# Sharing the last post norm between four engines, and loading x in smaller parts: one encoder layer on one core

## The chip, the cores and the metric

One core of one Trainium2 chip runs the kernel. The metric is the device time of one execution in microseconds (us), lower is better. TensorE is PE in the profile, VectorE is DVE, ScalarE is ACT, GpSimd is POOL, and SyncE, which only issues DMAs here, is SP. ACT issues some DMAs too.

## What is computed

```python
def layer_norm(x, g, b):               # over the last axis, float32, eps 1e-5
    mu, var = mean(x), mean((x - mu) ** 2)
    return (x - mu) * rsqrt(var + eps) * g + b

h = layer_norm(x, emb_ln_g, emb_ln_b)            # x: 256 tokens x 4096
p = h @ w_in                                     # 4096 x 13312
y_conv = c_b * centred_short_conv(c_c * c_h, conv_w) * silu(c_z)      # parts of p
y_attn = banded_window_attention(a_q, a_k, a_v, sink) * silu(a_z)     # parts of p
y = concat([y_conv, y_attn]) @ w_out             # 4096 x 4096
out = layer_norm(2 ** 0.25 * h + y, ln_g, ln_b)
```

## The kernel before

The 256 tokens are two tiles of 128, i = 0 and 1, with tokens on the partitions. The weights of both projections stream in as pieces of 1 MB; ACT rounds each to its high part (`split_hi`, L197), DVE subtracts to get the low part (`split_lo`, L201), and PE multiplies three times per piece (high by high, high by low, low by high).

**Prologue (L281 to L437).** x is loaded in parts of columns (`x_load`), and between the loads of the two tiles stand two pieces of w_in (`first`, `load(0)` and `load(1)`). DVE takes statistics per 512 columns (`stats`, L311), closes them (`stats_end`), normalises (`norm`, L319); PE turns the tiles (`transp`, L326, `transp2`, L344), ACT applies scale and shift (`turned1`, L332), and PE multiplies the turned x by the first two pieces in full float32 (`first_mm`, L361). All engines work through their instructions in the order in which the code issues them. On ACT the order is: the square root of tile 1, `split_hi(2)`, then `turned1(1, 0)`. On PE: the turns of tile 1 (L326, L344), then `first_mm(0, 1)`.

**The norm's small steps** are `small_chain` (L267 to L279): ACT takes a square root, DVE a reciprocal and one Newton step, and the last two instructions leave 1/sigma in `dst[.., 2]` and -mu/sigma in `dst[.., 3]`.

**The end (L978 to L992).** R (128 x 2 x 4096, in SBUF) holds alpha * h + y, and, for all chunks of columns that are done, already times ln_g (`end_out2`, L892). The last chunk has 256 columns; PE finishes it for tile 0 first, so that the norm of tile 0 runs while PE works on tile 1. For one tile: `finish_lhs` adds the residual, takes the statistics, calls `small_chain` and writes -mu/sigma, in a high and a low part and beside ones, to t5 (L900 to L905); `finish_tr` turns t5 on PE (L910) and copies it to lhs5 on ACT (L911); `finish_out` has, for each 512 columns, one matmul with 5 rows on PE that makes the shift -mu/sigma * ln_g + ln_b in PSUM (L918), and one instruction on DVE, R / sigma + shift (L919). Stores go out from L923 in pairs of 512 columns, the last two singly, from SP and ACT in turn.

`res_load` (L841 to L845) loads the rows that the residual of a chunk needs, for the last chunk into a tile z; it stands ahead of the load of the last piece of w_out.

Of the kernel before, what the change touches and what calls it, by code (L numbers as in the profile page):

```python
# [11 lines left out]
ALU = mybir.AluOpType  # L12
# [82 lines left out]
def encoder_kernel(ctx: ExitStack, tc: tile.TileContext, x, emb_g, emb_b, wi, ws, conv_w, sink, wo, ln_g, ln_b, out):  # L95
# [170 lines left out]

    def small_chain(dst, w):  # L267

        sd = small.tile([P, w], F32, name="sd", bufs=1)
        nc.scalar.activation(sd, dst[:, :, 1], AF.Sqrt, bias=eps_t)  # L270
        v = small.tile([P, w], F32, name="v", bufs=1)
        nc.vector.tensor_scalar(v, dst[:, :, 1], LN_EPS, -0.5, op0=ALU.add, op1=ALU.mult)
        y0 = small.tile([P, w], F32, name="y0", bufs=1)
        nc.vector.reciprocal(y0, sd)
        t = small.tile([P, w], F32, name="t", bufs=1)
        nc.vector.tensor_tensor(t, y0, y0, op=ALU.mult)
        nc.vector.tensor_tensor(t, t, v, op=ALU.mult)
        nc.vector.scalar_tensor_tensor(dst[:, :, 2], t, 1.5, y0, op0=ALU.add, op1=ALU.mult)
        nc.vector.scalar_tensor_tensor(dst[:, :, 3], dst[:, :, 0], -1.0, dst[:, :, 2], op0=ALU.mult, op1=ALU.mult)  # L279

    with tc.tile_pool(name="pro", bufs=1) as pro:  # L281
        warm = small.tile([P, 1], F32, name="sd", bufs=1)
        nc.scalar.activation(warm, eps_t, AF.Sqrt)
        xs = [pro.tile([P, D], F32, name=f"x{i}") for i in range(2)]
# [3 lines left out]

        def x_load(i):
            for c0, c1 in ((0, 1024), (1024, 2048), (2048, 3072), (3072, 3584), (3584, 4096)):  # L290
                nc.sync.dma_start(out=xs[i][:, c0:c1], in_=x[i * P:(i + 1) * P, c0:c1])

        first = [wpool.tile([P, PIECE], F32, name=f"first{j}", tag="whi") for j in range(2)]
# [13 lines left out]
        NQ = KT // 4  # L307
        st = [pro.tile([P, NQ, 6], F32, name=f"st{i}") for i in range(2)]

        def stats(i, c):  # L310
            nc.vector.bn_stats(st[i][:, c, :], xs[i][:, c * 512:(c + 1) * 512])  # L311

        def stats_end(i):
            nc.vector.bn_aggr(musd[:, i, 0:2], st[i])
            small_chain(musd[:, i:i + 1, :], 1)

# [40 lines left out]

        def first_mm(q, i):
            for k in range(PK):
# [8 lines left out]

        for c in range(NQ):
            stats(0, c)  # L370
# [13 lines left out]
        for c in range(NQ):  # L384
            stats(1, c)
        transp2(2, (0,))
        transp2(3, (0,))
        stats_end(1)
        split_hi(2)
# [409 lines left out]
    def open_p2():  # L799
        nonlocal p2, R, st2, ms2, rows, t5, lhs5  # L800
        ph.close()
        phs.close()
        p2 = ctx.enter_context(tc.tile_pool(name="p2", bufs=1))
        R = p2.tile([P, 2, D], F32, name="R")
        st2 = [p2.tile([P, ncs, 6], F32, name=f"s2{i}") for i in range(2)]
        ms2 = p2.tile([P, 2, 4], F32, name="ms2")
        rows = p2.tile([P, 3 * W], F32R, name="rows")
        t5 = p2.tile([P, 2, 72], F32, name="t5")
        nc.vector.memset(t5, 0.0)
        for b in (0, 32, 64):  # L810
# [19 lines left out]
    def res_load(n):  # L830
# [63 lines left out]
    def finish_lhs(n, i):  # L894
        r = end_out(n, i)
        nc.vector.bn_aggr(ms2[:, i, 0:2], st2[i])
        small_chain(ms2[:, i:i + 1, :], 1)
        ch = small.tile([P, 1], F32R, name="ch", bufs=1)
        c = ms2[:, i, 3:4]
        nc.vector.tensor_copy(ch, c)  # L900
        nc.vector.tensor_tensor(t5[:, i, 1:2], c, ch.bitcast(F32), op=ALU.subtract)
        for b in (0, 32, 64):
            if b:
                nc.vector.tensor_copy(t5[:, i, b + 1:b + 2], t5[:, i, 1:2])
            nc.vector.tensor_copy(t5[:, i, b:b + 3:2], ch.bitcast(F32).to_broadcast([P, 2]))  # L905
        end_out2(n, i, r)

    def finish_tr(i):
        tp = ps_att.tile([P, P], F32, name="att")
        nc.tensor.transpose(tp[0:72, :], t5[:, i, :], ident)  # L910
        nc.scalar.activation(lhs5[0:69, i, :], tp[0:69, :], AF.Copy)  # L911

    def finish_out(i, cs):
        for c in cs:
            sl = slice(c * 512, (c + 1) * 512)
            sh = (ps_att if c % 2 else ps_p).tile([P, 512], F32, name="att" if c % 2 else "pacc")
            b, k = RB[c]
            nc.tensor.matmul(sh, lhs5[b:b + 5, i, :], rows[b:b + 5, k * W:(k + 1) * W], start=True, stop=True)  # L918
            nc.vector.scalar_tensor_tensor(R[:, i, sl], R[:, i, sl], ms2[:, i, 2:3], sh, op0=ALU.mult, op1=ALU.add)  # L919
            if c % 2 == 1 and c < 7 or c >= 6:  # L920
                s0 = c if c >= 6 else c - 1
                sl = slice(s0 * 512, (c + 1) * 512)
                (nc.sync if c % 4 == 1 or c == 6 else nc.scalar).dma_start(out=out[i * P:(i + 1) * P, sl], in_=R[:, i, sl])  # L923

# [10 lines left out]
    for n, (c0, w, pk, j0) in enumerate(chunks):  # L935
        us = out_units(n)
        np_ = sum(u[0] == "opair" for u in us)
        for t, (kind, _, q) in enumerate(us):
# [40 lines left out]
    n = ncs - 1  # L979
    finish_lhs(n, 0)  # L980
# [9 lines left out]
    finish_lhs(n, 1)  # L990
    finish_tr(1)
    finish_out(1, range(8))  # L992
    pps.close()
# [51 lines left out]
```

## Time and profile before

| | us |
|---|---|
| median of 3 runs | 1544.9 (1544.02 to 1545.05) |
| the profiled execution | 1545.18 |
| its span, first to last instruction | 1543.4 |
| PE busy | 1522.7 |
| DVE busy | 1273.3 |
| ACT busy | 754.1 |
| POOL busy | 1.3, in 7 instructions |

The profiled execution is 1.8 us longer than its span and 0.3 us longer than the median. The busy time of PE is modelled, and a busy PE needs not be at its peak. "Idle before" in a row is the time in which the engine waited ahead of that group, and behind the arrow stands what ended it.

### The profile page before, as it was taken

Reading aid. Unit: us, or ns where it says so; the run is one execution under the profiler, and the core shown is the slowest. Engines: PE = TensorE matmul, PEld = TensorE weight load, DVE = VectorE, ACT = ScalarE, POOL = GpSimd, SP = SyncE. Lnnn points to the kernel's source line nnn. Section 1 sums busy time; section 2 is a strip of 40 time slices with the busy share of each in tenths; the row PEclk is TensorE's granted clock in tenths of the full one; section 3 lists DMA queues with packets and bytes.
Section 4 is the critical chain, followed back from the end, with each engine's and each line's share of the span. In section 5 each row is a group of like instructions: output and inputs, shape, how many; then the busy total and the mean of one; then the engine's idle time right before and its main releaser. Section 6 shows DMA issues by size and latency. Waiting matters only on the chain.

```text
span 1543.4 us, 21052 instructions
## 1 busy us (share of the span) xinstructions
PE 1522.7 (99%) x8622; PEld 1322.6 (86%) x8622; DVE 1273.3 (82%) x1454; ACT 754.1 (49%) x636; POOL 1.3 (0%) x7
## 2 busy tenths in 40 slices
PE   7999999999999999999999999999999999999997
PEld 4888888888888888888888888888888888888896
DVE  8678798888898888898888888888887688888666
ACT  4545556556465554544454445544555444444331
POOL 0000000000000000000000000000000000000000
PEclk9999999999999999999999999999999999999998
DMA  7535554545545456556555555566557655666752
GB/s 300 202 143 201 205 190 170 197 175 185 201 156 188 163 194 234 214 196 209 198 189 195 214 205 193 192 204 217 199 181 280 261 197 212 254 212 225 252 198 109
DMA packets 65951, 312.96 MB, mean 203 GB/s; under 512 B 7904, under 2 KB 11456, under 8 KB 41920
## 3 DMA queue, kind: packets, MB, share of 16 engines
q1 hardware_dynamic: 65280, 310.06, 56.4%
q8 instruction: 67, 1.10, 0.3%
q10 hardware_dynamic: 576, 1.57, 0.3%
q14 instruction: 28, 0.23, 0.0%
HBM read 303.66 MB, written 7.86 MB: 202 GB/s over the span
## 4 chain that ended last, share of the span: by engine, by line
PE 91%; DVE 4%; ACT 2%; issue 2%; DMA 1%; SPq 0%; DVEq 0%; ACTq 0%
PE acc L238 15%; PE acc L240 15%; PE acc L239 14%; PE acc L869 7%; PE acc L871 7%; PE acc L870 7%; PE pacc L263 4%; PE pacc L262 4%; PE pacc L264 4%; PE acc L263 3%; PE acc L262 3%; PE acc L264 3%; DVE wlo L201 2%; ACT whi L197 1%; PE att L470 1%
## 5 line engine op out<-in xcount | busy, mean ns | idle before, releaser
L197 ACT ACTIVATE whi<-w 128x2048 fp32r<-128x2048 f32 (+1 forms) x330 | 600.0, 1818 | 670.8 <-PE acc L240 288.8
L201 DVE TENSOR_TENSOR wlo<-w,whi 128x2048 fp32r<-128x2048 f32 (+1 forms) x330 | 712.1, 2164 | 197.8 <-ACT whi L197 196.0
L238 PE MATMUL acc<-whi,xT 128*128 128x512 f32 x1072 | 424.4, 396 | 0.0
L240 PE MATMUL acc<-whi,xT 128*128 128x512 f32 x1072 | 419.8, 392 | 0.0
L239 PE MATMUL acc<-wlo,xT 128*128 128x512 f32 x1072 | 417.7, 390 | 0.7 <-DVE wlo L201 0.7
L240 PEld LDWEIGHTS acc<-whi,xT 128*128 128x128 f32 x1072 | 201.3, 188 | 46.8
L239 PEld LDWEIGHTS acc<-wlo,xT 128*128 128x128 f32 x1072 | 201.4, 188 | 41.2 <-DVE wlo L201 1.0
L238 PEld LDWEIGHTS acc<-whi,xT 128*128 128x128 f32 x1072 | 201.5, 188 | 37.8
L869 PE MATMUL acc<-whi,xT 128*128 128x512 f32 (+1 forms) x496 | 182.9, 369 | 0.0
L871 PE MATMUL acc<-whi,xT 128*128 128x512 f32 (+1 forms) x496 | 181.8, 366 | 0.0
L870 PE MATMUL acc<-wlo,xT 128*128 128x512 f32 (+1 forms) x496 | 180.5, 364 | 0.0
L178 DVE TENSOR_TENSOR w<-w 128x512 f32<-128x512 f32 x154 | 105.3, 683 | 5.2 <-DMA w<-in_ws 5.2
L871 PEld LDWEIGHTS acc<-whi,xT 128*128 128x128 f32 x496 | 93.0, 188 | 16.8
L870 PEld LDWEIGHTS acc<-wlo,xT 128*128 128x128 f32 x496 | 93.1, 188 | 15.5
L869 PEld LDWEIGHTS acc<-whi,xT 128*128 128x128 f32 x496 | 93.2, 188 | 14.3 <-issue 0.4
L263 PE MATMUL acc<-wlo,xT 128*128 128x256 f32 x320 | 89.4, 279 | 0.0
L262 PE MATMUL acc<-whi,xT 128*128 128x256 f32 x320 | 89.3, 279 | 0.0
L264 PE MATMUL acc<-whi,xT 128*128 128x256 f32 x320 | 89.1, 278 | 0.0
L262 PE MATMUL pacc<-whi,xT 128*128 128x256 f32 x304 | 86.9, 286 | 0.0
L263 PE MATMUL pacc<-wlo,xT 128*128 128x256 f32 x304 | 84.9, 279 | 0.0
L264 PE MATMUL pacc<-whi,xT 128*128 128x256 f32 x304 | 84.7, 279 | 0.0
L263 PE MATMUL pacc<-wlo,SC 128*128 128x256 f32 x288 | 81.0, 281 | 0.0
(222 smaller groups left out, 1868.1 us busy)
## 6 DMA issues: line engine op xcount, KB each, us to landing
w<-in_wi SPq DMA_DIRECT2D x134, 1024.0 KB
w<-in_ws SPq DMA_DIRECT2D x154, 512.0 KB
w<-in_wo SPq DMA_DIRECT2D x43, 1024.0 KB
R<-in_wo SPq DMA_DIRECT2D x13, 1024.0 KB
yl<-yd SPq DMA_DIRECT2D x7, 512.0 KB
xc<-in_x SPq DMA_DIRECT2D x14, 256.0 KB
x<-in_x SPq DMA_DIRECT2D x6, 512.0 KB
R<-in_ws SPq DMA_DIRECT2D x6, 512.0 KB
```

The source lines that it names most:

```text
L178: nc.vector.tensor_tensor(s01, b22, b12.to_broadcast([P, 2, HW]), op=ALU.add)
L197: nc.scalar.activation(part(j, wh[j]), part(j, raw[j]), AF.Copy)
L201: nc.vector.tensor_tensor(part(j, wl[j]), part(j, raw[j]), part(j, wh[j]).bitcast(F32), op=ALU.subtract)
L238: nc.tensor.matmul(a, xh, hk, start=(first and k == 0), stop=False)
L239: nc.tensor.matmul(a, xh, lk, start=False, stop=False)
L240: nc.tensor.matmul(a, xl, hk, start=False, stop=(last and k == PK - 1))
L262: nc.tensor.matmul(o, ah, hi[:, w, :], start=(opens and p == 0), stop=False)
L263: nc.tensor.matmul(o, ah, lo[:, w, :], start=False, stop=False)
L264: nc.tensor.matmul(o, al, hi[:, w, :], start=False, stop=(closes and last))
L869: nc.tensor.matmul(o, yh, hk, start=first, stop=False)
L870: nc.tensor.matmul(o, yh, lk, start=False, stop=False)
L871: nc.tensor.matmul(o, yl, hk, start=False, stop=last)
```

## The change

- `small_chain` works on one column, takes the reciprocal of the square root on ACT in one instruction, and has three dependent instructions on DVE behind it where there were five.
- Prologue: x is loaded in seven parts per tile (two of 1024, three of 512, two of 256 columns) instead of five; the second piece of w_in goes in two halves, one behind the first 2048 columns of tile 1, one behind all of them. The statistics of the last 512 columns are taken in two halves. `first_mm(1, 0)` is split around the turns `transp2(2)` and `transp2(3)` of tile 0.
- End: the first 512 columns of both tiles need no matmul any more: their ln_g and ln_b are loaded, broadcast over the partitions, into z, and DVE works out shift and output (`finish_first`), for tile 1 in halves of 256. For tile 1 POOL instead of DVE writes t5 (four instructions). ACT writes a diagonal matrix of 1/sigma, and for columns 1024 to 2560 (blocks 2, 3 and 4) PE multiplies it with R in full float32 and adds the shift in the same PSUM bank, ACT copies the result and stores it (`finish_turned`). Blocks 1, 5, 6, 7 stay with DVE. Stores are of 512 columns each. `end_out2` of the last chunk comes later.

```diff
-    def small_chain(dst, w):
-        sd = small.tile([P, w], F32, name="sd", bufs=1)
-        nc.scalar.activation(sd, dst[:, :, 1], AF.Sqrt, bias=eps_t)
-        v = ...; y0 = ...
-        nc.vector.reciprocal(y0, sd)
-        nc.vector.tensor_tensor(t, y0, y0, op=ALU.mult)
-        nc.vector.tensor_tensor(t, t, v, op=ALU.mult)
+    def small_chain(i, dst):
+        nc.scalar.activation(y, dst[:, i, 1:2], AF.Abs_reciprocal_sqrt, bias=eps_t)
+        nc.vector.tensor_scalar(v, dst[:, i, 1:2], LN_EPS, -0.5, op0=ALU.add, op1=ALU.mult)
+        nc.vector.scalar_tensor_tensor(t, y, v, y, op0=ALU.mult, op1=ALU.mult)
...
-            for c0, c1 in ((0, 1024), (1024, 2048), (2048, 3072), (3072, 3584), (3584, 4096)):
+        X_PARTS = (0, 1024, 2048, 2560, 3072, 3584, 3840, 4096)
...
-        x_load(0)
+        x_load(0, 0, 7)
...
         load(0, first[0])
-        load(1, first[1])
-        x_load(1)
+        x_load(1, 0, 2)
+        first_load(0)
+        x_load(1, 2, 7)
+        first_load(1)
...
+        S_PARTS = [c * 512 for c in range(NQ)] + [D - 256, D]
...
-            first_mm(q, 0)
+        first_mm(0, 0)
+        first_mm(1, 0, 0, 2)
...
         transp2(3, (0,))
+        first_mm(1, 0, 2, 4)
...
+            g1, b1, t1 = (z[:, 5 * w + k * W:5 * w + (k + 1) * W] for k in range(3))
+            first_cols.extend((g1, b1, t1, z[:, 5 * w + 3 * W:5 * w + 3 * W + P]))
+            nc.sync.dma_start(out=g1, in_=bcast(ln_g, 0, W))
+            nc.sync.dma_start(out=b1, in_=bcast(ln_b, 0, W))
...
+        if i:
+            nc.scalar.activation(first_cols[3], ident, AF.Copy, scale=ms2[:, i, 2:3])
...
+        eng = nc.gpsimd if i else nc.vector
+        eng.tensor_copy(ch, c)
+        b = ch.bitcast(F32).to_broadcast([P, 3])
+        eng.tensor_tensor(t5[:, i, :, 1], c.to_broadcast([P, 3]), b, op=ALU.subtract)
+        eng.tensor_copy(t5[:, i, :, 0], b)
+        eng.tensor_copy(t5[:, i, :, 2], b)
...
+    def finish_first(i):
+        w = HW if i else W
+        for a in range(0, W, w):
+            sl = slice(a, a + w)
+            g, b, t = (v[:, sl] for v in first_cols[:3])
+            nc.vector.scalar_tensor_tensor(t, g, ms2[:, i, 3:4], b, op0=ALU.mult, op1=ALU.add)
+            nc.vector.scalar_tensor_tensor(R[:, i, sl], R[:, i, sl], ms2[:, i, 2:3], t, op0=ALU.mult, op1=ALU.add)
+            store_out(i, 0, nc.sync, a, a + w)
...
+    def finish_turned(i, c):
+        o = ps_acc.tile([P, W], F32, name="acc")
+        sl = slice(c * W, (c + 1) * W)
+        nc.tensor.matmul(o, first_cols[3], R[:, i, sl], start=True, stop=False)
+        finish_sh(i, c, o, False)
+        nc.scalar.activation(R[:, i, sl], o, AF.Copy)
+        store_out(i, c, nc.scalar)
...
     finish_tr(0)
+    end_out2(n, 0, r0)
+    finish_first(0)
     mm_out(last_mm + 2, n, (1,), 0, 2)
-    finish_out(0, range(0, 4))
+    finish_out(0, range(1, 4))
...
     finish_tr(1)
-    finish_out(1, range(8))
+    finish_first(1)
+    finish_out(1, (1, 5))
+    finish_turned(1, 2)
+    finish_out(1, (6,))
+    finish_turned(1, 3)
+    end_out2(n, 1, r1)
+    finish_out(1, (7,))
+    finish_turned(1, 4)
```

## Rows read from the trace of the kernel before

**Rows 1.** The page, part 1: busy time, share of the span, instructions.

```profile
PE 1522.7 (99%) x8622; PEld 1322.6 (86%) x8622; DVE 1273.3 (82%) x1454; ACT 754.1 (49%) x636; POOL 1.3 (0%) x7
```

**Rows 2.** The chain that ended last, in the prologue: start us, us, what.

```profile
22.99 1.11 PE acc L326 x8
...
24.56 3.51 PE acc L361 x8
```

**Rows 3.** Timeline of the prologue, DVE and ACT: start us, us, instruction, idle before.

```profile
7.84 2.47 DVE L311 BATCH_NORM_STATS2 st<-x 128x6 f32<-128x512 f32 x4 [0.80 <-DMA x<-in_x]
...
22.05 1.92 ACT L197 ACTIVATE whi<-w 128x2048 fp32r<-128x2048 f32 x1 [0.55 <-DMA w<-in_wi]
...
23.87 2.89 ACT L332 ACTIVATE hT<-acc,b_c,g_c 128x128 f32<-128x128 f32 x8
```

**Rows 4.** Windows: busy us of each engine, granted PE clock, DMA share, GB/s.

```profile
18.00:20.00 2.00, 2.00 (x6) 0.84 (x5) 2.00 (x4) 0.00 (x0) 0.00 (x0) 1.00 1.06 424
...
1498.00:1500.00 2.00, 2.00 (x19) 2.00 (x18) 0.00 (x0) 1.08 (x1) 0.00 (x0) 1.00 1.06 339
...
1504.00:1506.00 2.00, 2.00 (x19) 2.00 (x18) 0.96 (x3) 1.43 (x1) 0.00 (x0) 1.00 0.04 16
```

**Rows 5.** Timeline of SP and of ACT around the last weights.

```profile
1499.33 0.38 SPq L153 DMA_DIRECT2D w<-in_wo  x1
...
1506.40 1.90 ACT L197 ACTIVATE w<-w 128x2048 fp32r<-128x2048 f32 x1
```

**Rows 6.** The chain that ended last, at the end.

```profile
1522.32 0.42 PE pacc L918
...
1523.20 0.32 PE acc L869
...
1531.18 0.17 DVE t L276
...
1531.77 0.17 DVE ms L279
...
1532.76 0.44 PE att L910
...
1533.55 0.79 PE pacc L918
...
1534.38 4.04 DVE R L919 x6
```

**Rows 7.** Timeline of SP and of ACT: the first and the last store of tile 1.

```profile
1535.82 0.33 SPq L923 DMA_DIRECT2D out<-R  x1
...
1539.77 0.34 ACTq L923 DMA_DIRECT2D out<-R  x1
```

**Rows 8.** Windows of the end, columns as in group 4.

```profile
1530.00:1532.00 2.00, 0.00 (x0) 0.00 (x0) 1.52 (x9) 0.30 (x1) 0.00 (x0) 0.79 0.67 249
...
1536.00:1537.00 1.00, 1.00 (x2) 0.41 (x2) 1.00 (x2) 0.00 (x0) 0.00 (x0) 0.50 0.40 160
...
1542.00:1543.00 1.00, 0.00 (x0) 0.00 (x0) 0.00 (x0) 0.00 (x0) 0.00 (x0) 0.50 0.01 2
```

**Rows 9.** Timeline of the prologue, PE: full float32 matmuls, two records each.

```profile
8.63 3.74 PE L374 MATMUL att<-x,ident 128*128 128x512 f32 x4 [8.63 <-DMA x<-in_x]
...
13.80 7.13 PE L361 MATMUL acc<-first,hT 128*128 128x512 f32 x16
```

**Rows 10.** Timeline of POOL.

```profile
0.80 0.20 POOL L211 MEMSET ident<- 128x128 f32 x1 [0.29 <-POOLq L1034]
1.08 0.29 POOL L212 TENSOR_SCALAR_AFFINE_SELECT ident<-ident 128x128 f32<-128x128 f32 x1
```

**Rows 11.** DVE with operands in SBUF (timeline), ACT out of PSUM (groups by form).

```profile
1513.17 0.48 DVE L851 SCALAR_TENSOR_TENSOR z<-z,musd 128x256 f32<-128x256 f32 x1
1513.68 0.48 DVE L853 SCALAR_TENSOR_TENSOR z<-z,musd 128x256 f32<-128x256 f32 x1
...
L503 ACT ACTIVATE zT<-att 128x512 f32<-128x512 f32 x8 | 4.6, 578 | 0.0
```

More of the change, by code (lines that the diff above doesn't have):

```diff
@@ L287, in encoder_kernel, with x_load, first_load @@
         b_c = pro.tile([P, KT], F32, name="b_c")
-        def x_load(i):
-            for c0, c1 in ((0, 1024), (1024, 2048), (2048, 3072), (3072, 3584), (3584, 4096)):
+        X_PARTS = (0, 1024, 2048, 2560, 3072, 3584, 3840, 4096)
+        def x_load(i, k0, k1):
+            for c0, c1 in zip(X_PARTS[k0:k1], X_PARTS[k0 + 1:]):
                 nc.sync.dma_start(out=xs[i][:, c0:c1], in_=x[i * P:(i + 1) * P, c0:c1])
+        def first_load(h):
+            sl = slice(h * PIECE // 2, (h + 1) * PIECE // 2)
+            nc.sync.dma_start(out=first[1][:, sl], in_=wi[IN_PIECES.index(steps[1][1:])][:, sl])
         first = [wpool.tile([P, PIECE], F32, name=f"first{j}", tag="whi") for j in range(2)]
-        x_load(0)
+        x_load(0, 0, 7)
         nc.sync.dma_start(out=g_c, in_=emb_g)
@@ L307, in encoder_kernel @@
         NQ = KT // 4
-        st = [pro.tile([P, NQ, 6], F32, name=f"st{i}") for i in range(2)]
+        S_PARTS = [c * 512 for c in range(NQ)] + [D - 256, D]
+        st = [pro.tile([P, NQ + 1, 6], F32, name=f"st{i}") for i in range(2)]
         def stats(i, c):
-            nc.vector.bn_stats(st[i][:, c, :], xs[i][:, c * 512:(c + 1) * 512])
+            nc.vector.bn_stats(st[i][:, c, :], xs[i][:, S_PARTS[c]:S_PARTS[c + 1]])
         def stats_end(i):
             nc.vector.bn_aggr(musd[:, i, 0:2], st[i])
-            small_chain(musd[:, i:i + 1, :], 1)
+            small_chain(i, musd)
         def norm(i, q):
@@ L356, in encoder_kernel, with first_mm @@
             acc[0, i] = ps_acc.tile([P, W], F32, name="acc")
-        def first_mm(q, i):
-            for k in range(PK):
+        def first_mm(q, i, k0=0, k1=PK):
+            for k in range(k0, k1):
                 kt = q * PK + k
@@ L367, in x_split @@
             nc.vector.tensor_tensor(xT[:, sl, S:2 * S], hT[:, sl, :], xT[:, sl, 0:S].bitcast(F32), op=ALU.subtract)
-        for c in range(NQ):
+        for c in range(NQ + 1):
             stats(0, c)
@@ L380, in encoder_kernel @@
             turned1(0, q, t0[q])
-            first_mm(q, 0)
+        first_mm(0, 0)
+        first_mm(1, 0, 0, 2)
         for q in range(2, NQ):
             norm(0, q)
-        for c in range(NQ):
+        for c in range(NQ + 1):
             stats(1, c)
@@ L911, in finish_tr, with store_out @@
         nc.scalar.activation(lhs5[0:69, i, :], tp[0:69, :], AF.Copy)
+    def store_out(i, c, eng=None, a=0, b=W):
+        sl = slice(c * W + a, c * W + b)
+        (eng or (nc.scalar if c % 2 else nc.sync)).dma_start(out=out[i * P:(i + 1) * P, sl], in_=R[:, i, sl])
+    def finish_first(i):
[6 more added lines that the diff above has]
+            store_out(i, 0, nc.sync, a, a + w)
@@ L913, in finish_out, with finish_sh @@
+    def finish_sh(i, c, sh, start=True):
+        b, k = RB[c]
+        nc.tensor.matmul(sh, lhs5[b:b + 5, i, :], rows[b:b + 5, k * W:(k + 1) * W], start=start, stop=True)
     def finish_out(i, cs):
         for c in cs:
-            sl = slice(c * 512, (c + 1) * 512)
+            sl = slice(c * W, (c + 1) * W)
             sh = (ps_att if c % 2 else ps_p).tile([P, 512], F32, name="att" if c % 2 else "pacc")
-            b, k = RB[c]
-            nc.tensor.matmul(sh, lhs5[b:b + 5, i, :], rows[b:b + 5, k * W:(k + 1) * W], start=True, stop=True)
+            finish_sh(i, c, sh)
@@ L919, in finish_out @@
             nc.vector.scalar_tensor_tensor(R[:, i, sl], R[:, i, sl], ms2[:, i, 2:3], sh, op0=ALU.mult, op1=ALU.add)
[L920 to L923, printed above, removed]
+            store_out(i, c, nc.sync if i else None)
+    def finish_turned(i, c):
+        o = ps_acc.tile([P, W], F32, name="acc")
+        sl = slice(c * W, (c + 1) * W)
+        nc.tensor.matmul(o, first_cols[3], R[:, i, sl], start=True, stop=False)
+        finish_sh(i, c, o, False)
+        nc.scalar.activation(R[:, i, sl], o, AF.Copy)
+        store_out(i, c, nc.scalar)
@@ L971, in encoder_kernel @@
                 rows_split()
-                nc.scalar.activation(small.tile([P, 1], F32, name="sd", bufs=1), eps_t, AF.Sqrt)
+                nc.scalar.activation(small.tile([P, 1], F32, name="sd", bufs=1), eps_t, AF.Abs_reciprocal_sqrt)
             if n == ncs - 2 and t == 0:
@@ L979, in encoder_kernel @@
     n = ncs - 1
-    finish_lhs(n, 0)
+    r0 = finish_lhs(n, 0)
     mm_out(last_mm, n, (1,))
```

33 lines of the change are left out of this document (13 added, 20 removed).

## The prediction

> **What bounds the kernel now.** I read the page's busy times first, then the chain that ended last, once for the prologue and once for the end, then the timeline around the steps that the diff touches, and the windows for the clock and the DMA. PE is busy for 1522.7 of 1543.4 us, in a stream that the change does not touch between about 33 and 1515 us [rows 1]. So only two stretches can move the time: the one before PE's stream closes up, and the one after its last matmul.
>
> In the prologue the reader is to see that PE is without a gap from the turns of tile 1, at 22.99, and that `first_mm(0, 1)` follows at 24.56 [rows 2]. What stands ahead of that on DVE is a wait of 0.80 us for a part of x, and on ACT a wait of 0.55 us for a weight piece: `split_hi(2)` can start at 22.05 only, and `turned1(1, 0)`, which feeds `first_mm(0, 1)`, stands behind it in ACT's order and starts at 23.87 [rows 3].
>
> At the end the chain leaves PE and goes through small DVE steps, the turn of t5 at 1532.76, the 5-row matmul at 1533.55 and eight DVE instructions of 0.67 us from 1534.38 [rows 6]. Stores are issued between 1535.82 and 1539.77 [rows 7]. PE's clock is granted fully until about 1531.2 (mean 0.79 in 1530 to 1532) and then at half, the 1.2 GHz level, to the end; PE had had nothing to do since 1529.2 [rows 8].
>
> **Prologue, part by part.** Steps of the norm's chain follow each other on DVE every 0.20 us ((1531.77 - 1531.18) / 3) [rows 6]. Two fewer save 0.39 us per tile. The smaller x parts can take away at most the wait of 0.80 us [rows 3]; the last statistics in two halves cost between 0 and one more instruction of 0.62 us (2.47 / 4) per tile, and I take 0.1, since the elements are the same [rows 3]. DVE would so reach the norm of tile 1 between 0.3 and 1.6 us earlier, and PE's turns start earlier by as much.
>
> That gain is mostly not passed on. `first_mm(0, 1)` needs the first column block of `turned1(1, 0)`, that is 23.87 plus an eighth of 2.89 us, about 24.3, and that start hangs on the weight piece behind `split_hi(2)` [rows 3]. So with the piece landing as before, PE gains 24.56 - 24.3 = 0.25 us, and its idle time moves from ahead of the turns to behind them [rows 2, 3]. The bytes ahead of the piece are the same, in other order. But four parts of 256 columns (0.52 MB) now have rows of 1 KB: a stretch that loads such parts moves 339 GB/s, one that loads long rows 424, both with the DMA engines full [rows 4]. That is 1.55 - 1.24 = 0.31 us later; with a little for the halved weight piece 0.35. Prologue: -0.25 + 0.35 = +0.1 us, with bounds -0.3 (the piece lands as before) and +0.6. The second half of `first_mm(1, 0)` now waits for the last half piece, which is the last thing ahead of that same weight piece (1.05 MB, 2.5 us at 424 GB/s), so it lands at about 19.6 [rows 3, 4]; its four records of 0.45 us end at 21.4, before tile 1 can be turned: nothing, and one to one if it came 1 us later [rows 9].
>
> **Late loads.** ln_g and ln_b for the first columns put two DMAs of 256 KB on SP ahead of the last weight piece, issued at 1499.33 [rows 5]. At 339 GB/s they take 1.55 us of the DMA engines. The piece had landed by about 1504 (share 0.04 after that), and ACT splits it from 1506.40 [rows 4, 5]: some 0.9 us of cover stay. Nothing; beyond that a delay would reach PE.
>
> **Tile 0.** Four 5-row matmuls stand in PE's stream between 1522.32 and 1523.20, 0.22 us each [rows 6]. One falls away: -0.22 us. Its DVE work lies under PE's matmuls.
>
> **Tile 1, until lhs5 is ready.** The chain gives -0.39. The seven DVE steps of t5 took from 1531.94 to 1532.76, 0.82 us [rows 6]. Four POOL instructions take their place, and the trace shows POOL at no such work. Lower bound: POOL as fast as DVE, four sevenths, 0.47. Upper bound, unhindered: four times 0.29 plus a gap of 0.08, 1.5. I take the spacing of the only two dependent POOL instructions, 0.28 us, times four, 1.12, plus 0.05 to start [rows 10]. So the first 5-row matmul starts at 1533.55 - 0.39 - 0.82 + 1.17 = 1533.5, as before.
>
> During that time DVE runs `finish_first(1)`: four instructions on 256 columns with both tensors in SBUF, 0.51 us from start to start when dependent, 2.0 us in all [rows 11]. No row here shows POOL and DVE working side by side. The Trainium skill (page SBUF — State Buffer, section "SBUF: two separate sides") says that a DVE instruction with two SBUF inputs and a GpSimd instruction that reads SBUF exclude each other for the whole instruction; by it t5 would be finished 2.0 us later. It is a rival below.
>
> **Tile 1, after lhs5.** DVE has only four more outputs; PE has three full float32 matmuls and seven 5-row ones in one queue, and the last of each block decides. A float32 call is two records: 16 records in 7.13 us, so 0.89 us at the full clock, and twice that, 1.78, at half (four cold records took 3.74) [rows 9]. The 5-row ones take 0.22 and 0.44 [rows 6]. Sum: 3 x 1.78 + 7 x 0.44 = 8.4 us at half clock, 4.2 at full. The clock will be at half when this begins, as before [rows 8]. At the kernel's start PE worked densely from 8.63, at half pace for 3.74 us, and was at full pace from 13.80, so the clock rose 3.7 to 5.2 us after dense work began [rows 9]. I take 5.2: 5.2 + (8.4 - 5.2) / 2 = 6.8 us. The result then takes 0.35 us to leave PE (0.79 less 0.44) [rows 6] and ACT 0.58 us for 128 x 512 out of PSUM [rows 11]. So the last store is issued about 7.8 us after 1533.5, at 1541.3, where it was 1539.77: +1.55 us [rows 7].
>
> Before, the last store stood behind others: 1543.40 - 1539.77 = 3.63 us from its issue to the end. Alone it needs 0.78 us to begin (issue 1535.82, data from about 1536.6), 0.66 us for 256 KB at 400 GB/s, and 1.4 us from the last byte at 1542.0 to the end: 2.84 [rows 7, 8]. That is -0.8. The smaller and earlier stores change nothing else, since none of them is late.
>
> **Sum.** +0.1 - 0.22 + 1.55 - 0.8 = +0.6 us on a profiled execution of 1545.18, whose median companion is 0.28 us lower: 1545.5.
>
> **The rivals.** (a) *PE's clock stays at half.* In the run before, PE worked from 1533.55 to 1537.9 and the grant stayed 0.50 [rows 8], though with gaps. Then the 8.4 us stand in full, 1.6 us more: 1547.1. For it: that row; against it: the work is now dense, as at the start [rows 9].
>
> (b) *POOL is shut out by DVE* (the slower end). t5 waits for `finish_first(1)`: 2.0 + 1.12 us instead of 1.12 [rows 10, 11], and since everything on PE stands behind lhs5 it goes to the end one to one: 1547.5. It makes the kernel slower than before as soon as t5 takes over 0.5 us, and slower by 0.2% (3.1 us) only from 3.6 us on, or from 2.0 if (a) holds too. For it: DVE's first instruction starts 0.03 us after the value that both wait for, POOL's later. Against it: nothing in this trace shows it. The skill's page above is the rule for it.
>
> (c) *The end gets shorter.* POOL at its lower bound (-0.65), the clock up after 3.7 us (-0.75), the weight piece as before (-0.35): 1543.8. Here the change does what it is laid out for.
>
> (d) *The prologue's gain is passed on whole*, since the piece lands earlier too: up to 1 us less than the sum, 1544.4. Against it: the same bytes stand ahead of the piece.
>
> **How the numbers follow.** Forecast 0.45, (a) 0.2, (b) 0.2, (c) and (d) 0.15. The range reaches from a little below (c) to a little above (b), 1543.5 to 1547.9. About 0.2% (3.1 us) is what a measurement of this kernel can tell from no change. Slower by more needs (a) and (b) together, 1549.1: 0.08. Faster by more needs a clock that never falls (-2.6) and (c): 0.03. The rest, 0.89, is the same.
>
> **What would show it.** ACT's `split_hi(2)` should start at 22.2 to 22.6, `turned1(1, 0)` right behind it, and PE should be idle ahead of `first_mm(0, 1)` instead of ahead of the turns. Four 5-row matmuls should be three for tile 0. At the end PE should be without gaps from lhs5 on, with the float32 records at 0.89 us and later 0.45, and the last store should be ACT's, of block 4, some 1.5 us later than before, with an idle DMA ahead of it. The prediction is wrong in its prologue if that ACT start moves by over half a us; in its end, if the four POOL instructions span over 1.6 us or under 0.6, if the granted clock is not back before the end, or if DVE's stores end last.

## The result: 5.35 us slower, and the profile after

| | before | after |
|---|---|---|
| median, us | 1544.9 (1543.88 to 1545.75) | 1550.25 (1548.75 to 1551.49) |
| ratio, 95% interval | | 1.0036 [1.0021, 1.0050] |
| profiled execution, span | 1545.18, 1543.4 | 1551.49, 1549.8 |

The forecast was 1545.5, with a range up to 1547.9, and 0.08 on slower by more than 0.2%. The spans differ by 6.3 us. Three readings divide that: the first matmul of L238, where PE's long stream begins, the end of the last real matmul, and the end of the span. In the rest of the document E is that end of the last real matmul.

| us | before | after | difference |
|---|---|---|---|
| start to the first L238 matmul | 32.57 | 34.37 | +1.80 |
| from there to E | 1496.63 | 1497.50 | +0.87 |
| from E to the end of the span | 14.23 | 17.90 | +3.67 |

**The prologue.** The timeline of after around 22 us (start, duration, engine, line, operation; in brackets the idle time before and what ended it), which answers to [rows 2, 3]:

```profile
21.38 1.98 PE L367 MATMUL acc<-first,hT 128*128 128x512 f32 x4 [1.09 <-DMA first<-in_wi]
...
23.20 1.04 PE L332 MATMUL acc<-ident,x 128*128 128x128 f32 x8
23.85 1.91 ACT L197 ACTIVATE whi<-w 128x2048 fp32r<-128x2048 f32 x1 [2.32 <-DMA w<-in_wi]
...
25.67 2.89 ACT L338 ACTIVATE hT<-acc,b_c,g_c 128x128 f32<-128x128 f32 x8
...
26.16 3.70 PE L367 MATMUL acc<-first,hT 128*128 128x512 f32 x8 [1.49 <-ACT hT L338]
```

The shape is the forecast one: `split_hi(2)` (L197) waits for its weight piece, `turned1(1, 0)` (L338) stands behind it on ACT, and PE, which has turned tile 1 early enough, is idle for 1.49 us ahead of `first_mm(0, 1)`. Only the size is off: 23.85 where 22.2 to 22.6 was forecast, from 22.05 before. The second half piece of `first` was late as well: PE waited for it for 1.09 us, until 21.38, where 19.6 was forecast. DVE began to normalise tile 1 at 22.09 instead of 22.40, the least of the forecast gain, since it now waited 0.69 us for a part of x of tile 1. PE's turns (23.20) were still done ahead of the ACT copy that they feed (25.67).

**The end.** The timeline of after on POOL and DVE, from the value that the shift needs (written by 1534.26):

```profile
1534.10 0.40 ACT L911 ACTIVATE z<-ident,ms 128x128 f32<-128x128 f32 x1 [0.48 <-DVE ms L275]
1534.29 0.48 DVE L937 SCALAR_TENSOR_TENSOR z<-z,ms 128x256 f32<-128x256 f32 x1
1534.55 0.27 POOL L915 CAST ch<-ms 128x1 fp32r<-128x1 f32 x1 [1462.86 <-ACT z L911]
1534.81 0.48 DVE L938 SCALAR_TENSOR_TENSOR R<-R,ms,z 128x256 f32<-128x256 f32 x1
1534.91 0.44 POOL L917 TENSOR_TENSOR t<-ms,ch 128x3 f32<-128x3 f32 x1
1535.21 0.48 DVE L937 SCALAR_TENSOR_TENSOR z<-z,ms 128x256 f32<-128x256 f32 x1
1535.30 0.45 POOL L918 COPY t<-ch 128x3 f32<-128x3 f32 x1
...
1535.68 0.18 POOL L919 COPY t<-ch 128x3 f32<-128x3 f32 x1
1535.73 0.48 DVE L938 SCALAR_TENSOR_TENSOR R<-R,ms,z 128x256 f32<-128x256 f32 x1
1535.92 0.15 PEld L924 LDWEIGHTS att<-ident,t 128*96 128x96 f32 x1 [4.25 <-POOL t L919]
```

POOL's first instruction starts 0.29 us after the value is there; the trace puts that to ACT's diagonal. The next ones show POOL and DVE beside each other: each of the first three ends about 0.06 us after DVE's instruction of the moment (1534.77, 1535.29, 1535.69), and the one that started ahead of DVE's took 0.18 us. From the value to the turn on PE it is 1.66 us, where seven DVE steps took 0.82 [rows 6].

The chain of after that ended last, from there on (start, time, what it stood on):

```profile
1536.73 0.79 PE att L943 x2
1537.52 2.00 PE acc L957 x2
1539.53 0.72 PE acc L943
...
1544.98 0.73 PE acc L943
1545.74 0.60 ACT R L959
```

And the windows of the same stretch (busy time and count of each engine, then the granted clock, the DMA share and GB/s), with the row of the last store's issue under them:

```profile
1534.00:1536.00 2.00, 0.08 (x1) 0.08 (x1) 1.86 (x6) 0.40 (x1) 1.23 (x4) 0.54 0.00 0
...
1538.00:1545.00 7.00, 7.00 (x11) 1.66 (x9) 2.79 (x5) 1.19 (x2) 0.00 (x0) 0.50 0.48 179
...
1546.36 0.34 ACTq L929 DMA_DIRECT2D out<-R  x1
```

PE works without a gap from 1536.73 to 1545.7 and does all of it at the 1.2 GHz level: the grant is 0.50 in every window up to the end. A float32 matmul (two records) is 2.00 us on the chain. The 5-row matmuls stand between them mostly in pairs that start within 0.01 us of each other, 0.72 or 0.79 us for a pair. The last store is issued at 1546.36 instead of 1539.77 [rows 7].

### The profile page after: what moved, and what is told of

It is laid out like the page before. It is cut to its first block, busy times and chain, and to the rows that moved or that the text cites. A ratio compares the mean times of both kernels' runs of the same rounds, so it can differ in the third digit from the quotient of the medians.

```text
span 1549.8 us, 21083 instructions
## 1 busy us (share of the span) xinstructions
PE 1528.1 (99%) x8626; PEld 1323.3 (85%) x8626; DVE 1271.6 (82%) x1437; ACT 756.5 (49%) x640; POOL 2.5 (0%) x11
## 4 chain that ended last, share of the span: by engine, by line
PE 92%; ACT 2%; DVE 2%; issue 2%; DMA 2%; SPq 0%; POOL 0%; POOLq 0%; ACTq 0%
PE acc L238 15%; PE acc L240 15%; PE acc L239 15%; PE acc L881 7%; PE acc L883 7%; PE acc L882 7%; PE pacc L263 4%; PE pacc L262 4%; PE pacc L264 4%; PE acc L263 3%; PE acc L262 3%; PE acc L264 3%; ACT whi L197 1%; DVE wlo L201 1%; DMA w<-in_wi 1%
## 5 line engine op out<-in xcount | busy, mean ns | idle before, releaser
L197 ACT ACTIVATE whi<-w 128x2048 fp32r<-128x2048 f32 (+1 forms) x330 | 600.1, 1819 | 674.2 <-PE acc L240 293.8
L238 PE MATMUL acc<-whi,xT 128*128 128x512 f32 x1072 | 424.5, 396 | 0.0
L238 PEld LDWEIGHTS acc<-whi,xT 128*128 128x128 f32 x1072 | 201.6, 188 | 38.3
```

Of the source, the lines that this page charges most:

```text
L197: nc.scalar.activation(part(j, wh[j]), part(j, raw[j]), AF.Copy)
L238: nc.tensor.matmul(a, xh, hk, start=(first and k == 0), stop=False)
```

## The experiments

"Before" beside a median is the kernel before in the same batch, and a kernel is placed against the change by how far each is above its own before: the change is 5.35 us above. Positions are those of each kernel's own profiled execution.

### The two halves of the change by themselves

`head_only`: the kernel before with the new prologue alone. `tail_only`: the kernel before with the new small chain and the new end alone.

> The kernel before with the new prologue alone: seven parts per tile of x, the second weight piece in halves behind them, the statistics in nine pieces, first_mm(1, 0) split. Old small_chain and old end. Theory A (the prologue costs by itself: the weight piece behind split_hi(2) lands late and turned1(1, 0) waits behind it): split_hi(2) starts at 23.5 to 24 instead of 22.05, PE's first L238 matmul 1.5 to 2 us later than 32.6, and 1546.4 to 1546.9 us. Rival B (the 1.8 us of the changed kernel's prologue were a chance of one execution): split_hi(2) within 0.4 us of 22.05 and 1544.5 to 1545.3 us.

> The kernel before with the new small_chain and the new end; the prologue's loads as before. Theory A (the end costs 3.5 us by itself, since PE works its float32 matmuls and 5-row matmuls off at 1.2 GHz): from the last matmul of the last chunk to the end 17.7 to 18.1 us, where it was 14.2, and 1548.0 to 1548.8 us; prologue within 0.3 us of before. Rival B (most of the loss sits in the prologue or in the stretch between): 1545.5 to 1546.5 us.

Measured: `head_only` 1546.21, before 1545.38, ratio 1.0007 [0.9998, 1.0017]. `tail_only` 1549.46, ratio 1.0026 [1.0015, 1.0037]; from E to the end 17.6 us. So most of the loss is in the end. `head_only` lies between its two expectations, in its time as in the start of `split_hi(2)`. The prologue's share can't be told by medians (0.2% is 3.1 us), but the trace of `head_only` shows it at its place, in the timeline of ACT and PE:

```profile
23.02 1.92 ACT L197 ACTIVATE whi<-w 128x2048 fp32r<-128x2048 f32 x1 [1.47 <-DMA w<-in_wi]
...
25.33 2.41 PE L370 MATMUL acc<-first,hT 128*128 128x512 f32 x5 [0.72 <-ACT hT L341]
```

Its first L238 matmul starts 0.96 us later than before's, and that of `tail_only`, with the old loads, 0.18.

### The clock: spare matmuls behind the last real one

```diff
+    spare = ps_p.tile([P, 512], F32, name="pacc")
+    for _ in range(16):
+        nc.tensor.matmul(spare, xT[:, 0, 0:P], xT[:, 0, :], start=True, stop=True)
     r1 = finish_lhs(n, 1)
```

> The changed kernel with 16 spare matmuls (128 x 128 by 128 x 512, result not used) on PE right behind its last matmul of the last chunk, so that PE is not idle while DVE and POOL prepare the norm of tile 1. Theory A (the end is long because the clock is at half there): the granted clock stays at 1.00 through most of the end, the float32 records take about 0.45 us instead of 1.0, and the last store is issued 4 to 5 us earlier: 1545.0 to 1546.5 us. Rival B (the 5-row and float32 matmuls keep the clock down or the path through ACT and the stores decides): the records still take 0.9 to 1.0 us and the time is 1549 to 1550.5 us.

Measured: 1546.14, before 1545.38, 1.0006 [0.9997, 1.0015]: 0.8 us above before, 4.6 less than the change. Its timeline and windows of the end:

```profile
1536.79 1.12 PE L957 MATMUL acc<-R,z 128*128 128x512 f32 x2
...
1538.00:1540.00 2.00, 2.00 (x7) 0.75 (x8) 1.47 (x4) 0.73 (x2) 0.00 (x0) 1.00 0.77 284
```

The clock stays granted in full, a float32 pair takes 1.12 us instead of 2.08, the distance from pair to pair is 1.49 instead of 2.73, and the last store of ACT is issued at 1541.97. So the half clock is worth 4.6 of the change's 5.35 us. No other single edit that leaves PE its share of the work won as much; taking the share away (`dve_alone`, below) won the same.

### Why the clock didn't come back

The forecast had taken from the kernel's start that dense work brings the clock back. Three kernels ask what in the end's dense work differs. `late_dense` puts eight spare float32 matmuls on 128 rows between the turn of t5 and the first 5-row matmul, `late_thin` 24 spare 5-row matmuls at the same place, and `full_rows` keeps number, order and columns of the change's matmuls but gives 128 rows to the 5-row ones of blocks 2 to 7 (they read a tile of y, so the shift of these blocks is left out). The edits in this order, the last one inside `finish_sh`:

```diff
     finish_tr(1)
+    for _ in range(8):
+        nc.tensor.matmul(spare, first_cols[3], R[:, 1, 2 * W:3 * W], start=True, stop=True)
...
+    for _ in range(24):
+        nc.tensor.matmul(spare, lhs5[0:5, 0, :], rows[0:5, 0:W], start=True, stop=True)
...
+        if i and c > 1:
+            nc.tensor.matmul(sh, xT[:, 0, 0:P], xT[:, 0, :], start=start, stop=True)
+            return
```

> The change with 8 spare float32 matmuls of 128 rows and 512 columns between the turn of t5 and the first 5-row matmul, where the clock is at half: 8 x 1.78 = 14.2 us at half clock if it stays there. It is about the clock alone; the time gets worse by 7 to 14 us. If dense work on all 128 rows brings the clock back as at the kernel's start (3.7 to 5.2 us after it began), the granted clock is 1.0 again from about E+9 on, the spare records go from 1.78 to 0.89 us a call and the float32 and 5-row matmuls behind them run at full pace. If the clock doesn't come back in this end at all, every spare call takes 1.78 to 2.08 us and the grant is 0.50 to the last matmul.

> The change, with the 5-row matmuls of tile 1's blocks 2 to 7 replaced by matmuls of 128 rows with the same 512 columns (on a tile of y, so the shift of these blocks is left out and replaced by something else); block 1 keeps its own, so all of it starts as in the change. Same number of matmuls, same columns, same order. Theory: the 5-row matmuls kept the clock at half. Then the granted clock is 1.0 again 4 to 5.5 us after the first float32 matmul (1537.45 in the change), about 1541.5 to 1543, the third float32 pair takes about 1.12 instead of 2.08, and the last ACT copy starts 1.0 to 2.0 us earlier than in the change (E + 12 to 13 instead of E + 13.9). Rival: the rows don't matter and the stretch is too short or broken up; then the records stay at 2.08 and the copy starts at E + 13.9.

> The change with 24 spare 5-row matmuls of 512 columns (on tile 0's lhs5) between the turn of t5 and the first 5-row matmul of tile 1, where late_dense had 128-row ones: 24 x 0.44 = 10.6 us at half clock, without gaps. Theory: 5-row matmuls don't bring the clock back; the grant stays 0.50 through them, and the end is 10 to 11 us longer than the change's. Rival: it is only the dense time that counts; then the grant is 1.0 about 5 us after they begin, the later spares go at 0.22, the float32 pairs behind them at 1.12, and the end is only about 10.6 - 2.8 - 3.8 = 4 us longer than the change's.

`late_dense`, timeline (the spares and two of their weight loads) and windows:

```profile
1535.90 9.28 PE L1033 MATMUL pacc<-R,z 128*128 128x512 f32 x16
...
1540.17 0.32 PEld L1033 LDWEIGHTS pacc<-R,z 128*128 128x128 f32 x1 [0.52 <-issue]
1540.73 0.19 PEld L1033 LDWEIGHTS pacc<-R,z 128*128 128x128 f32 x1 [0.24 <-issue]
...
1538.00:1540.00 2.00, 2.00 (x3) 0.67 (x2) 0.00 (x0) 0.00 (x0) 0.00 (x0) 0.50 0.00 0
1540.00:1542.00 2.00, 2.00 (x5) 0.89 (x4) 0.00 (x0) 0.00 (x0) 0.00 (x0) 0.89 0.00 0
```

`full_rows`, timeline of PE and windows:

```profile
1536.36 0.79 PE L944 MATMUL att<-xT 128*128 128x512 f32 x1
1536.95 1.91 PE L960 MATMUL acc<-R,z 128*128 128x512 f32 x2
...
1539.51 1.12 PE L960 MATMUL acc<-R,z 128*128 128x512 f32 x2
...
1538.00:1539.00 1.00, 1.00 (x3) 0.47 (x2) 0.00 (x0) 0.00 (x0) 0.00 (x0) 0.50 0.91 334
1539.00:1540.00 1.00, 1.00 (x3) 0.61 (x2) 0.25 (x1) 0.60 (x1) 0.00 (x0) 0.65 0.51 191
1540.00:1541.00 1.00, 1.00 (x5) 0.64 (x4) 0.83 (x2) 0.11 (x1) 0.00 (x0) 1.00 0.21 76
```

`late_thin`, timeline of PE and windows (22 of the spares; the other two stand among the change's own matmuls):

```profile
1535.00 9.59 PE L1033 MATMUL pacc<-rows,lhs 5*128 5x512 f32 x22
...
1540.00:1544.00 4.00, 4.00 (x12) 3.00 (x12) 0.00 (x0) 0.00 (x0) 0.00 (x0) 0.50 0.00 0
1552.00:1554.00 2.00, 2.00 (x3) 0.28 (x1) 0.14 (x1) 0.00 (x0) 0.00 (x0) 0.50 0.59 221
```

With 128 rows in every matmul the clock came back. In `late_dense` it rises between two weight loads, at 1540.17 and 1540.73, some 4.5 us after the spares began. In `full_rows`, with the change's own columns, the window 1539 to 1540 has a mean of 0.65, so the rise is near 1539.7, 3.3 us after the first 128-row matmul and sooner than expected, and the pair at 1539.51 took 1.12. In `late_thin` PE has nothing but 5-row matmuls without a gap from 1535.0 to 1545.8, then 8 us of the change's own mix, and the grant, which falls to 0.50 at 1535.2, stays there to the end.

`late_dense` took 1555.86, `late_thin` 1559.83 and `full_rows` 1548.04, one execution each; from E to the end 22.5, 27.4 and 15.1 us, and the change 17.9. So `late_thin` is 9.5 us longer than the change, near the 10 to 11 of the theory and far from the 4 of its rival. The spares of `late_dense` differ from those of `late_thin` in the type too (float32 in two records against one), so the comparison that changes the rows alone is `full_rows` with the change. There the clock also fell later (mean 1.00 in 1534 to 1536, where the change has 0.54), so not all of its 2.8 us come from the rise. That the late fall doesn't bring the rise with it can be read in `t5_dve` (below), which has the change's own matmuls: there too the clock fell only after PE had begun on its share, and no window behind it is above 0.50:

```profile
1534.00:1536.00 2.00, 1.80 (x4) 0.48 (x4) 1.96 (x5) 0.14 (x1) 0.00 (x0) 0.73 0.20 66
...
1540.00:1542.00 2.00, 2.00 (x3) 0.49 (x3) 0.70 (x1) 0.52 (x1) 0.00 (x0) 0.50 0.34 126
```

The Trainium skill (page TensorE: Matmul & The Clock Gate, section "Part 1: The HAM clock gate (the "warmup" mystery)") says that the clock is set by how busy PE has been recently. The windows of `late_dense` agree; those of `late_thin` don't: there PE is busy throughout by the profile (4.00 of 4.00 us) and keeps half clock, and here the measurement decides.

### The turned matmuls ahead of lhs5

`turned_early`: the three float32 matmuls are taken away from the 5-row ones that they are joined with and issued earlier, the first ahead of the turn of t5, the second right behind it, the third behind the end of block 2.

```diff
+    o2 = turned_mm(1, 2)
     finish_tr(1)
+    o3 = turned_mm(1, 3)
     finish_first(1)
     finish_out(1, (1, 5))
-    finish_turned(1, 2)
+    turned_end(1, 2, o2)
+    o4 = turned_mm(1, 4)
```

> The changed kernel with its float32 matmuls split from their 5-row ones: the one of block 2 goes ahead of the turn of t5, that of block 3 right behind it, that of block 4 behind the first 5-row matmuls. They need only 1/sigma, so PE starts about 2 us earlier. Theory A (dense float32 work does not bring the clock back within the end; only work in the idle time counts): granted clock 0.50 to the end, float32 records still 0.85 to 1.0 us, last store 2 to 2.6 us earlier, 1547.7 to 1548.4 us. Rival B (denser float32 work, as at the start of the kernel, lifts the clock after 3.7 to 5.2 us): granted clock back at 1.00 around 8 us after the last matmul of the last chunk, 1546.5 to 1547.5 us.

Measured: 1547.67, before 1545.09, 1.0016 [1.0007, 1.0025], 2.8 us less than the change. E to the end took 16.15 us. The timeline of PE and a window of the end:

```profile
1532.85 1.12 PE L955 MATMUL acc<-R,z 128*128 128x512 f32 x2 [2.68 <-ACT z L911]
...
1534.46 1.92 PE L955 MATMUL acc<-R,z 128*128 128x512 f32 x2
...
1538.00:1540.00 2.00, 2.00 (x4) 0.50 (x4) 0.54 (x1) 0.15 (x1) 0.00 (x0) 0.50 0.64 240
```

The first pair still runs at full clock and fills PE's idle time; the grant then falls and stays at 0.50 for the rest. So the time is won by the place, not by a clock that came back.

### t5 by DVE

`t5_dve`: `eng = nc.vector` for both tiles.

> The changed kernel with t5 of tile 1 written by DVE (the four small instructions ahead of finish_first) instead of POOL. Theory A (POOL costs 1.6 us where DVE needs 0.5, and half of POOL's time is waiting for DVE's instructions on SBUF): the first 5-row matmul starts 3.7 to 3.9 us after the last matmul of the last chunk instead of 4.86, and 1549.0 to 1549.4 us. Rival B (DVE's own outputs or ACT decide the end, or the wait for lhs5 is hidden): no change, 1549.9 to 1550.5 us.

Measured: 1548.63, before 1545.09, 1.0024 [1.0014, 1.0034], 1.8 us less than the change. The timeline:

```profile
1533.31 0.16 DVE L919 COPY t<-ch 128x3 f32<-128x3 f32 x1
...
1534.20 0.50 PE L943 MATMUL att<-rows,lhs 5*128 5x512 f32 x2 [0.36 <-ACT lhs L925]
```

t5 now takes 0.50 us (1532.97 to 1533.47), and the first 5-row matmul starts 3.65 us after E instead of 4.86. The last store of ACT comes 1.8 us earlier after E than in the change, 0.6 more than that, since the first matmuls still met the full clock.

### No share for PE and ACT

`dve_alone`: the change, but blocks 1 to 7 of tile 1 stay with DVE.

```diff
     finish_first(1)
-    finish_out(1, (1, 5))
-    finish_turned(1, 2)
...
+    end_out2(n, 1, r1)
+    finish_out(1, range(1, 8))
```

> The change, except that blocks 1 to 7 of tile 1 all stay with VectorE: no float32 matmuls, no copies by ACT, and the scaling by ln_g (end_out2) ahead of the outputs. Theory: the share given to PE and ACT costs more at half clock than VectorE's four outputs save. Then the first 5-row matmul is as in the change (about E+4.9), the outputs follow each other at 0.67 us as before, seven of them 4.7, the last store is issued at about E+10.5 instead of E+14.5, and the kernel takes about 1546.2, 4 us less than the change. Rival: the end is bound by what comes late anyway (t5, the stores' way out); then it is less than 1.5 us faster than the change.

Measured: 1546.32, before 1545.71, 1.0005 [0.9996, 1.0014], 4.7 us less than the change; E to the end 13.91 us. The first and the last of the seven outputs:

```profile
1537.16 0.75 DVE L950 SCALAR_TENSOR_TENSOR R<-R,ms,att 128x512 f32<-128x512 f32 x1 [1.01 <-PE att L943]
...
1541.12 0.74 DVE L950 SCALAR_TENSOR_TENSOR R<-R,ms,att 128x512 f32<-128x512 f32 x1
```

DVE does all seven in 4.7 us, 0.66 from start to start, and is done 5.5 us after the first 5-row matmul, where PE in the change is busy for 9.0 us from there. At half clock the share itself is what made the end slow. At full clock it is no gain either as the change places it: `spare_matmuls` took 13.8 us from E to the end, `dve_alone` 13.9, and their medians stand 0.8 and 0.6 us above before.

### The prologue: ACT's order, the parts, the order of the loads

`act_order`: the change, with `split_hi(2)` moved behind `turned1(1, 1)`.

```diff
-        split_hi(2)
...
         turned1(1, 1, t1[1])
+        split_hi(2)
         first_mm(1, 1)
```

> The changed kernel with ACT's split_hi(2) moved behind turned1(1, 0) and turned1(1, 1). Theory A (the prologue is lost because the turned tile 1 waits on ACT behind a late weight piece): first_mm(0, 1) starts about 24.6 instead of 26.16, PE's first L238 matmul comes 1.3 to 1.6 us earlier than in the changed kernel, 1548.4 to 1549.1 us. Rival B (PE waits for the weight piece itself or for x): PE's first L238 matmul as in the changed kernel, 1549.8 to 1550.6 us.

`parts_only`: the kernel before, x in seven parts, nothing else. `order_only`: five parts, but the second weight piece in halves in the new places.

```diff
-            for c0, c1 in ((0, 1024), (1024, 2048), (2048, 3072), (3072, 3584), (3584, 4096)):
+            for c0, c1 in ((0, 1024), (1024, 2048), (2048, 2560), (2560, 3072), (3072, 3584), (3584, 3840), (3840, 4096)):
```

> The kernel before with x in seven parts per tile, and nothing else: the order of the loads, statistics and everything behind as before. Theory A (short rows and more DMAs cost): split_hi(2) starts 0.3 to 0.7 us later than 22.05. Theory B (the halves of the second weight piece and its place cost, not the parts): within 0.2 us of 22.05. Time 1545.0 to 1546.0 us in both.

> The kernel before with x in five parts as before, but the second weight piece in two halves, one behind the first 2048 columns of tile 1 and one behind all of it, and first_mm(1, 0) split. Theory A (short rows cost): split_hi(2) within 0.3 us of 22.05, 1545.0 to 1545.6 us. Theory B (the mixed order costs: DMA packets stall where x and the halves alternate): split_hi(2) starts at 22.8 to 23.8, first L238 matmul 0.5 to 1.5 us later than before, 1545.9 to 1546.9 us.

Measured: `act_order` 1548.87, before 1545.38, 1.0022 [1.0012, 1.0032], 1.9 us less than the change. `parts_only` 1545.98 and `order_only` 1545.99, before 1545.09, both 1.0005 [0.9996, 1.0015], which the medians can't tell apart. The starts of `split_hi(2)` in `parts_only` and `order_only`, and of `turned1(1, 0)` and `first_mm(0, 1)` in `act_order`:

```profile
23.23 1.92 ACT L197 ACTIVATE whi<-w 128x2048 fp32r<-128x2048 f32 x1 [0.77 <-DMA w<-in_wi]
```

```profile
22.39 1.92 ACT L197 ACTIVATE whi<-w 128x2048 fp32r<-128x2048 f32 x1 [1.56 <-DMA w<-in_wi]
```

```profile
23.46 2.90 ACT L338 ACTIVATE hT<-acc,b_c,g_c 128x128 f32<-128x128 f32 x8 [1.85 <-PE acc L332]
...
24.18 3.60 PE L367 MATMUL acc<-first,hT 128*128 128x512 f32 x8
```

The windows from 2 to 22 us of before, `parts_only` and after, in this order:

```profile
2.00:22.00 20.00, 12.86 (x36) 5.91 (x36) 15.89 (x36) 3.78 (x12) 0.00 (x0) 1.00 1.01 389
```

```profile
2.00:22.00 20.00, 12.63 (x36) 5.90 (x36) 15.58 (x32) 3.48 (x11) 0.00 (x0) 1.00 1.01 379
```

```profile
2.00:22.00 20.00, 11.56 (x34) 5.54 (x35) 15.90 (x35) 3.78 (x12) 0.00 (x0) 1.00 1.00 364
```

With the DMA engines equally full, fewer bytes had moved by 22 us: 20 x 10 = 0.2 MB less with the parts alone, 20 x 25 = 0.5 MB less in the change. At 410 GB/s, the rate of `parts_only` from 22 to 24 us, these are 0.5 and 1.2 us, of the 1.18 and 1.80 us by which `split_hi(2)` starts later than at 22.05 [rows 3]. In these single profiles the smaller parts cost more (+1.18) than the order (+0.34); what makes up the rest beside the rate was not found. Other kernels with the change's loads and ACT order started `split_hi(2)` at 22.89 (`turned_early`) to 23.59 (`t5_dve`), so the change's own profile, 23.85, is the late end of a spread of 1 us. That is more than the parts and the order differ by, so which of the two costs more is not shown. And none of it reaches PE once `turned1(1, 0)` doesn't stand behind it: in `act_order` the first L238 matmul is at 32.28, 0.3 us before before's.

### The causes mended together

`mended`: the change with `split_hi(2)` behind `turned1(1, 1)`, t5 by DVE, 12 spare matmuls behind the last real one, and each float32 matmul of tile 1 ahead of the 5-row matmuls of the block before, all behind the turn of t5. `mended_old_loads`: the same with the loads of the kernel before.

> As mended_old_loads, but with the loads of the change (seven parts of x, the second weight piece in halves). If split_hi(2)'s place was all that the new loads cost, it is within 0.3 us of that kernel (act_order's first L238 matmul came 0.3 us earlier than before's), about 1542.6. If the smaller parts cost something by themselves that ACT's order doesn't cover, it is 0.8 to 1.5 us slower than mended_old_loads.

> The new end with the loads of the kernel before, split_hi(2) behind the first two copies of turned1, t5 of tile 1 by VectorE, 12 spare matmuls of 512 columns behind the last real one (2.6 us at 0.22), and each float32 turn issued one place ahead of the 5-row matmul that it is joined with. If the three causes found so far (ACT's order in the prologue, the clock at half, GpSimd's t5) are the whole loss, the first L238 matmul comes 0.3 to 0.5 us before that of the kernel before, and the end, counted from the last real matmul, is E+2.9 (t5) + 0.7 (lhs5) + 3 x 0.9 + 7 x 0.22 + 0.9 to the issue of the last ACT store = E+8.8, then 3.4 to the end: E+12.2 against E+14.2 before. With the 0.22 us of tile 0 that is -2.6 us: 1542.5. If another loss remains (the rest of the stream, between 33 and 1515 us), the time stays at 1544 to 1545 although these places are mended. A clock that falls in spite of the spare work would give about 1547.

Measured: `mended` 1543.22 (1542.91 to 1544.48), before 1545.71, 0.9984 [0.9975, 0.9993]; `mended_old_loads` 1543.88, 0.9989 [0.9980, 0.9998]. Both are faster than the kernel before, by 2.5 and 1.8 us (0.16% and 0.11%), where some 2.6 was expected, and the new loads of x and `first` cost nothing that shows any more: the first L238 matmul comes at 31.74 and 31.81, 0.8 us before that of the kernel before. From E to the end it takes 12.8 and 12.7 us, where 12.2 was expected; E is the end of the last real matmul, 1528.65 in `mended`. Its last copy by ACT and the window around it:

```profile
1536.50 0.60 ACT L960 ACTIVATE R<-acc 128x512 f32<-128x512 f32 x1 [0.88 <-PE acc L943]
...
1536.00:1538.00 2.00, 0.44 (x3) 0.12 (x2) 0.81 (x2) 0.60 (x1) 0.00 (x0) 1.00 1.03 376
```

The DMA engines are full (share 1.03) while PE ends and behind it, and from that copy's end, 1537.10, to the end of the span, 1541.5, it is 4.4 us where the change has 3.4: stores now queue, and they are what comes last.

One more loss shows in the stream ahead of E. In three profiles PE waits for the low part of the last weight piece, 1.50 us in `mended_old_loads`, 0.74 in `turned_early` and, most, in `dve_alone`:

```profile
1515.37 0.39 PE L882 MATMUL acc<-w,xT 128*128 128x256 f32 x1 [1.94 <-DVE w L201]
```

There DVE waited for ACT's split of the piece, and ACT 4.02 us for its DMA. Ahead of that DMA stand the late loads of ln_g and ln_b for the first columns. The other nine kernels with these loads, the change's own among them, show no such wait of over 0.1 us, and neither do the four kernels without them. No kernel with the rest of the end and without these loads was run, so that they are the cause is likely, not shown.

## Why the prediction was wrong

Its sum was +0.6 us, the spans differ by 6.3. Term by term, with the size that the trace of after gives:

| step of the prediction | forecast | after | missed by |
|---|---|---|---|
| prologue (first L238 matmul) | +0.1 | +1.8 | 1.7 |
| late loads of ln_g and ln_b | 0 | 0 | 0 |
| one 5-row matmul of tile 0 less | -0.22 | -0.22 | 0 |
| small chain | -0.39 | -0.34 | 0.05 |
| t5, from the value to the turn | 1.17 | 1.66 | 0.5 |
| first 5-row matmul to the last store's issue | 7.8 | 9.63 | 1.8 |
| the last store to the end | 2.84 | 3.4 | 0.6 |
| PE's stream in between, no step | 0 | +1.1 | 1.1 |

**The clock (failed, the largest).** The step "I take 5.2: 5.2 + (8.4 - 5.2) / 2" carried the rise at the kernel's start over to the end. The prediction held one thing alike in both, that PE is dense, and that is so. But at the start all matmuls have 128 rows, and in the end three pairs alternate with 5-row matmuls; `late_thin` and `full_rows`, with one execution each, show that this made the difference. The rival "PE's clock stays at half" was the case that came: it gave 8.4 us of PE work, measured 9.0, as a float32 pair at half clock is 2.00 us there and not 1.78 (the four cold records of [rows 9] give 1.87 a pair). Being the case with a row of the end itself [rows 8] behind it, it deserved more than 0.2. The cover that the prediction didn't price: with the clock at half, PE's share takes longer than DVE would need for the same blocks (`dve_alone`).

**The prologue (right in shape, mis-sized).** The place of the wait, the engine and the order were forecast; the term "0.35 us later" for the weight piece was not its size. It took the lower rate for the four smallest parts only, 0.52 MB. The trace shows a lower rate over the whole stretch, and the piece 0.8 to 1.8 us later in the kernels with these loads. The bound of +0.6 was too narrow. The second half piece of `first`, too, came some 1.8 us later than the sum had it, which cost nothing by itself here, as PE had to wait for ACT behind it in any case.

**POOL (right cause, too low a price).** The four instructions span 1.31 us (1534.55 to 1535.86), inside the 0.6 to 1.6 that the prediction allowed; 0.29 ahead of them and 0.06 behind them make 1.66. The estimate had 1.12 and 0.05. Whether POOL really waited for ACT's diagonal in those 0.29 us or starts slowly by itself was not tried. The rule of the Trainium skill (page SBUF — State Buffer, section "SBUF: two separate sides"), that such an instruction on either engine shuts the other out, is borne out in one direction: POOL's ends follow DVE's. But DVE ran on at its own 0.48 us, also where POOL's fourth instruction had begun 0.05 us ahead of it, and POOL lost at most 0.27 us (0.45 - 0.18) per instruction, since each of its own got in between two of DVE's. The 2.0 us of rival (b), in which all four of DVE's come first, did not appear.

**The last store.** 3.4 us from its issue to the end with the way free, not 2.84. The working had put together pieces of a stretch in which several stores flowed at once; the gain over before's 3.63 was 0.2, not 0.8.

**The rest.** PE's stream between 33 us and E, which the change doesn't touch but for the 0.22 us and the late loads, took 1496.45 to 1498.71 us in the 16 profiled kernels. Waits don't explain it: PE's idle time in it is 1.2 to 3.4 us (the most where the last weight piece was late), and without it 1494.6 to 1496.8 us are left. Before's profile (1496.63) and the change's (1497.50) have the same idle time. Some 1 us of the 6.3 is this, its cause stays open, and it is why the spans of two single profiles tell nothing under 2 us, while the stretches before 33 us and behind E can be compared.

## What to carry to other kernels

Work that was handed to TensorE behind its last large matmul ran here at the half level, for most of it or all, unless PE had been kept busy until then (`spare_matmuls`, `mended`) or had only matmuls of 128 rows (`late_dense`, `full_rows`), so price such work at the half level unless a row of that very stretch shows the rise, and compare that price with what the freed engine would have needed. A clock rise read elsewhere in the trace carries over only if the matmuls are alike. Before splitting a load into smaller parts, look for what stands in order behind the last of them: here moving one ACT instruction brought the first L238 matmul 0.8 us forward with the old loads (31.81), and the new loads added 0.1 (31.74).

## What the runs showed of the hardware

- Gapless 5-row matmuls of 512 columns left the granted clock at 0.50 for 10.6 us (`late_thin`); with 128 rows and the same columns 1.00 came after 3.3 us (`full_rows`) and 4.5 us (`late_dense`).
- 2.9 and 3.8 us of spare matmuls behind the last real one (12 and 16) kept it at 1.00 until PE was done, 5-row matmuls included (`mended`, `spare_matmuls`).
- A POOL copy on 128 x 3 took 0.18 us when it began ahead of DVE's instruction, and the same copy 0.45 when DVE's was on its way; DVE's took 0.48 either way (`after`).
- Sixteen kernels with the same long stream of PE, some 1497 us, differ by up to 2.3 us in it at full clock, and by 2.2 with PE's idle time taken out.
